# Product-key expert layer: four u tiles a head, v tiles prepared before the u sweep ends, first head's low parts off GpSimd

## The chip, the cores and the metric

The kernel runs on one core of one Trainium2 chip. The metric is the device time of one execution in microseconds. The core has a matrix engine (TensorE, PE in the rows; PEld is its weight load), VectorE (DVE), ScalarE (ACT), GpSimd (POOL) and a queue engine (SP) that issues most transfers; GpSimd issues the indirect ones (gathers).

## The reference

Two layers over 512 tokens of width 1024. Each layer has a mixer (convolution and gated linear attention, or forgetting attention) and then an expert part, which is what the change touches:

```python
q = (h @ wq).reshape(B, S, PEER_HEADS, 2, half)            # 8 heads, 2 halves of 128
s1, s2 = q[..., 0, :] . keys[:, 0], q[..., 1, :] . keys[:, 1]   # 128 scores each
v1, i1 = lax.top_k(s1, 16); v2, i2 = lax.top_k(s2, 16)
cand = (v1[..., :, None] + v2[..., None, :])               # 256 sums
sc, j = lax.top_k(cand, 16)
e1 = take(i1, j // 16); e2 = take(i2, j % 16)
experts = e1 * 128 + e2; gates = softmax(sc)
act = gelu(einsum('td,ted->te', ht, u[et]))                # 16384 experts, 128 used by a token
out = einsum('te,ted->td', gt * act, v[et])
```

## The kernel before, in words

The expert part computes three of the four token blocks densely: all 128 tiles of 128 experts of `u` against the tokens (the u sweep), then all 128 tiles of `v` (the v sweep), with a matrix G that holds each token's gate at its experts and zero elsewhere. Block 0 and the first 32 tokens of block 1 use gathers of single rows instead (`g_u`, `g_v`, and `x_u` for the 32 tokens). Each weight tile is loaded in float32 (`weight`, SP queue, 512 KB), ScalarE rounds it to a high part (L52), and the rest is subtracted into a low part (L53), on VectorE or, where `eng` says so, on GpSimd. Each product is three matmuls (L75 to L77).

The stages of an expert part, in order:

- the norm (`rms_body`): squares on ScalarE, a power on GpSimd (L104), the scaled rows on VectorE (L105), transposes on PE (L112);
- the route stage, a loop over 8 heads: two projections (`proj_T`), scores, then `route`, all top-16 searches on VectorE (`topk`, L740 to L745), then `WQU` = 3 u tiles (`u_step`). The last part of routing, `lookup`, turns positions into expert numbers with one-hot sums (L798 to L807); it is put one head later, behind the first u tile's low part. Every head past the first puts `XR` = 2 gathers `x_u` in motion, the last one 4. After the eighth head `gates` makes the softmax and E holds the expert numbers. GpSimd makes the low parts of both projections of head 0, of the second projection of every head, of u tiles 0 and 1, and of the odd u tiles from 13 on within this stage;
- the rest of the u sweep, 104 tiles: first `flip` transposes E and the gates on PE (L929), then every tile comes with one `gate4` of the 96 that build G (GpSimd, ScalarE and VectorE make one-hot rows, PE multiplies them, L959, and a copy goes to G in DRAM) and about 1.4 gathers. The gates end `TAIL` = 8 tiles before the end;
- the v sweep, 128 tiles: G is read back in pieces of eight tiles (`gc`, 1.5 MB), multiplied by the activations (L1083), split (`wh`, `wl`) and multiplied with `v` on PE (L1053). The first tile's preparation follows the last u tile and the gelu of the gathered dots (`g_w`).

A tile planner takes the program and sets each engine's order by a simulated time line; `issue_after(x)` puts instructions behind x on x's engine. Buffers bound how far one engine runs ahead: 4 raw tiles, 3 high and 3 low parts, 5 gathered rows.

Of the kernel before, what the change touches and what calls it, by code (L numbers as in the profile page):

```python
# [32 lines left out]
XR = 2  # L33
# [7 lines left out]
WQU = 3  # L41
# [5 lines left out]
class Trunk:  # L47
# [8 lines left out]
    def weight(self, src, shape=None, eng=None):  # L56
# [6 lines left out]
        self.split(raw, hi, lo, eng)  # L63
# [29 lines left out]
    def rms_body(self, rp, i, hT, h0, order, after, hx):  # L93
# [3 lines left out]
        def scale(b):  # L97
# [4 lines left out]
            nc.scalar.activation(sq, self.xb[b], AF.Square, accum_out=ss)  # L102
# [30 lines left out]
    def proj_T(self, src, hT, eng=None, between=None):  # L133

        wh, wl = self.weight(src, (KD, P), eng)
# [611 lines left out]
    def route(self, sb, s, E, SC, hd):  # L747
# [21 lines left out]
        def lookup():  # L769
# [4 lines left out]
            dx = sb.tile([P, 2, n, TOPK], BF16, name="dx")  # L774
            ixw = ix.rearrange("p b w k -> p w b k")
            for w in range(2):
                nc.vector.tensor_tensor(dx[:, w], ixw[:, w, :, 1:], ixw[:, w, :, 0:TOPK], op=ALU.subtract)
            wide = [P, 2 * n, TOPK, TOPK]
            st = sb.tile([P, 2 * n, TOPK * TOPK], BF16, name="st", tag="rs", bufs=2)
            nc.scalar.activation(st.rearrange("p b (r k) -> p b r k", k=TOPK),  # L780
                                 dx.rearrange("p w b r -> p (w b) r")[:, :, :, None].to_broadcast(wide), AF.Copy)
            jf = sb.tile([P, n, TOPK], F32, name="jf")
            nc.vector.tensor_copy(jf, j)


            pl = sb.tile([P, 2, n, TOPK], BF16, name="pl")
            nc.scalar.activation(pl[:, 0], jf, AF.Copy)
            bits = sb.tile([P, 3, n, TOPK], U32, name="bits")
            j2 = sb.tile([P, 3, n, TOPK], F32, name="j2")
            for k, (m, end) in enumerate(((3, 56.0), (4, 40.0), (8, 16.0))):  # L790
                nc.vector.tensor_scalar(bits[:, k], j, m, None, op0=ALU.bitwise_and)
                nc.vector.scalar_tensor_tensor(j2[:, k], jf, end, bits[:, k], op0=ALU.is_lt, op1=ALU.mult)
            nc.vector.tensor_tensor(j2[:, 0], j2[:, 0], j2[:, 1], op=ALU.add)
            nc.vector.tensor_tensor(pl[:, 1], j2[:, 0], j2[:, 2], op=ALU.add)

            oh = sb.tile([P, 2 * n, TOPK * TOPK], BF16, name="oh", tag="rs", bufs=2)
            for w in range(2):
                nc.vector.tensor_tensor(oh[:, w * n:(w + 1) * n].rearrange("p b (r k) -> p b r k", k=TOPK),  # L798
                                        pl[:, w, :, None, :].to_broadcast([P, n, TOPK, TOPK]),
                                        self.steps[:, w, None].to_broadcast([P, n, TOPK, TOPK]), op=ALU.is_ge)  # L800
            nc.vector.tensor_tensor(oh, oh, st, op=ALU.mult)

            for m in (1, 2, 4):
                pair = oh.rearrange("p b (r h m) -> p b r h m", h=2, m=m * TOPK)
                nc.vector.tensor_tensor(pair[:, :, :, 0, 0:TOPK], pair[:, :, :, 0, 0:TOPK], pair[:, :, :, 1, 0:TOPK],
                                        op=ALU.add)
# [417 lines left out]
```

## Time and profile before

| | us |
|---|---|
| median of 3 runs | 3182.42 |
| lowest and highest run | 3172.59, 3187.05 |
| profiled execution, its own time | 3180.49 |
| span in the profile | 3178.7 |
| PE busy | 3024.8 |
| DVE busy | 2466.8 |
| ACT busy | 1541.1 |
| POOL busy | 1394.1 |

The span runs from the first instruction to the last. Busy times overlap between engines. Matmuls are pipelined, and a busy PE at half of its clock still counts as busy, so the share of 95% does not by itself say that nothing is to be had. "Granted clock" is the share of PE's full 2.4 GHz.

### The profile page before, as it was taken

The page shows a single profiled execution, that of the slowest core. Times are in us where ns is not written, and L with a number is a line of the kernel's source. Part 1 is how long each engine was busy: PE and PEld are TensorE (multiplying, and loading weights), DVE is VectorE, ACT ScalarE, POOL GpSimd, SP SyncE. Part 2 cuts the span into 40 slices and gives each one's busy share as a digit, 9 for nine tenths or more (in the row PEclk, how much of TensorE's full clock was granted, in tenths as well). Part 3 has the DMA queues.
Part 4 walks back from the last instruction along what each step waited for, and adds up shares of the span by engine and source line. Part 5 has one row for each costly group of instructions (what it writes and reads, how often), then busy time and mean ns, then how long its engine had stood idle before and what let it go on. Part 6 is the DMA issues. An engine that isn't in the chain of part 4 may idle for free.

```text
span 3178.7 us, 46471 instructions
## 1 busy us (share of the span) xinstructions
PE 3024.8 (95%) x15934; PEld 2635.8 (83%) x15934; DVE 2466.8 (78%) x5338; ACT 1541.1 (48%) x2668; POOL 1394.1 (44%) x1072
## 2 busy tenths in 40 slices
PE   8999996999999999999999989969999999999999
PEld 6767886999999888887766669869999997887787
DVE  7764999888787888888546538998877888888886
ACT  4353334777765333333356624337667753333333
POOL 1321233999786233333100012328999983332330
PEclk9999997999999999999999999989999999999999
DMA  4104554999999999999421125558999999999996
GB/s 154 60 27 131 178 182 137 344 368 357 338 336 337 323 355 359 346 358 346 149 80 43 39 83 178 166 181 293 340 347 330 342 340 332 369 354 336 361 346 211
DMA packets 343808, 815.00 MB, mean 256 GB/s; under 512 B 27897, under 2 KB 182922, under 8 KB 337426
## 3 DMA queue, kind: packets, MB, share of 16 engines
q1 hardware_dynamic: 260626, 510.00, 46.2%
q0 software_dynamic: 82944, 302.03, 26.8%
q8 instruction: 125, 2.05, 0.3%
q14 instruction: 113, 0.93, 0.1%
HBM read 717.74 MB, written 93.06 MB: 255 GB/s over the span
## 4 chain that ended last, share of the span: by engine, by line
PE 74%; DVE 8%; DMA 2%; ACT 1%; issue 1%; POOL 0%; SPq 0%; DVEq 0%; ACTq 0%; POOLq 0%
PE acc L1053 32%; PE pu L75 9%; PE pu L77 9%; PE pu L76 9%; PE bank L959 5%; PE bank L77 2%; PE bank L75 2%; PE bank L76 2%; PE po L672 1%; PE bank L640 1%; DVE wlo L53 1%; DVE gr L897 1%; DVE tk L743 1%; DMA raw<-in_vF_dram 1%; ACT whi L52 1%
## 5 line engine op out<-in xcount | busy, mean ns | idle before, releaser
L52 ACT ACTIVATE whi<-raw 128x1024 fp32r<-128x1024 f32 x604 | 634.7, 1056 | 643.2 <-PE pu L76 310.6
L53 DVE TENSOR_TENSOR wlo<-raw,whi 128x1024 fp32r<-128x1024 f32 x565 | 693.0, 1227 | 194.8 <-ACT whi L52 193.8
L75 PE MATMUL pu<-hhi,whi 128*128 128x352 f32 x2048 | 687.1, 335 | 13.3 <-ACT xact L871 10.2
L77 PE MATMUL pu<-hhi,wlo 128*128 128x352 f32 x2048 | 671.8, 328 | 12.9 <-DVE wlo L53 11.9
L76 PE MATMUL pu<-hlo,whi 128*128 128x352 f32 x2048 | 669.3, 327 | 0.6 <-DVE hlo L115 0.6
L914 POOL DMA_INDIRECT gr<-in_vF_dram,ids x256 | 329.6, 1287 | 664.0 <-DVE x L916 620.2
L1053 PE MATMUL acc<-wlo,wh 128*128 128x512 f32 x1536 | 474.4, 390 | 0.0
L1053 PE MATMUL acc<-whi,wl 128*128 128x512 f32 x1536 | 471.7, 389 | 0.0
L1053 PE MATMUL acc<-whi,wh 128*128 128x512 f32 x1536 | 430.7, 392 | 24.1 <-ACT wh L52 13.8
L52 ACT ACTIVATE wh<-gc 128x384 fp32r<-128x384 f32 x256 | 134.2, 525 | 644.5 <-PE acc L1053 628.0
L879 POOL DMA_INDIRECT gr<-in_uN_dram,ids x256 | 406.3, 1587 | 83.3 <-issue 37.1
L942 POOL TENSOR_SCALAR a<-cst,sT 128x128 f32<-128x128 f32 x384 | 425.7, 1118 | 38.2 <-ACT sT L930 19.3
L75 PEld LDWEIGHTS pu<-hhi,whi 128*128 128x128 f32 x2048 | 391.6, 191 | 17.8 <-ACT xact L871 12.7
L77 PEld LDWEIGHTS pu<-hhi,wlo 128*128 128x128 f32 x2048 | 390.5, 191 | 14.4 <-DVE wlo L53 13.1
L76 PEld LDWEIGHTS pu<-hlo,whi 128*128 128x128 f32 x2048 | 391.5, 191 | 1.7 <-DVE hlo L115 0.9
L1053 PEld LDWEIGHTS acc<-whi,wh 128*128 128x128 f32 x1536 | 288.7, 189 | 88.4 <-ACT whi L52 14.6
L1053 PEld LDWEIGHTS acc<-wlo,wh 128*128 128x128 f32 x1536 | 289.8, 189 | 60.3
L1053 PEld LDWEIGHTS acc<-whi,wl 128*128 128x128 f32 x1536 | 288.6, 188 | 59.9
L916 DVE SCALAR_TENSOR_TENSOR x<-gr,dots,x 128x1024 f32<-128x1024 f32 x256 | 327.4, 1279 | 0.4
L881 DVE CUSTOM_DVE_ANT_0 gr<-gr,h 128x1024 f32<-128x1024 f32 x256 | 309.5, 1230 | 15.7 <-DMA gr<-in_uN_dram,ids 14.9
L53 POOL TENSOR_TENSOR wlo<-raw,whi 128x1024 fp32r<-128x1024 f32 x39 | 101.4, 2606 | 497.6 <-ACT whi L52 497.5
L53 DVE TENSOR_TENSOR wl<-gc,wh 128x384 fp32r<-128x384 f32 x256 | 141.9, 555 | 120.9 <-ACT wh L52 118.5
(264 smaller groups left out, 4529.4 us busy)
## 6 DMA issues: line engine op xcount, KB each, us to landing
raw<-in_uT_dram SPq DMA_DIRECT2D x256, 512.0 KB
raw<-in_vF_dram SPq DMA_DIRECT2D x256, 512.0 KB
G<-big SPq DMA_DIRECT2D x48, 1024.0 KB
gc<-G SPq DMA_DIRECT2D x32, 1536.0 KB
aside<-xact SPq DMA_DIRECT2D x208, 176.0 KB
at<-aside SPq DMA_DIRECT2D x104, 352.0 KB
raw<-in_w_in_dram SPq DMA_DIRECT2D x32, 512.0 KB
raw<-in_wq_dram SPq DMA_DIRECT2D x32, 512.0 KB
```

What stands on the lines that cost most here:

```text
L52: first = self.nc.scalar.activation(hi, raw, AF.Copy)
L53: self.last_lo = (eng or self.nc.vector).tensor_tensor(lo, raw, hi.bitcast(F32), op=ALU.subtract)
L75: mm(out, lh, rh, start=first, stop=False)
L76: mm(out, lh, rl, start=False, stop=False)
L77: return mm(out, ll, rh, start=False, stop=last)
L879: nc.gpsimd.indirect_dma_start(out=r, out_offset=None, in_=uN, in_offset=bass.IndirectOffsetOnAxis(ap=ids[:, s:s + 1], axis=0))
L881: return lambda: nc.vector.tensor_tensor_reduce(r, r, h0, 1.0, 0.0, ALU.mult, ALU.add, accum_out=dots[:, s:s + 1])
L914: nc.gpsimd.indirect_dma_start(out=r, out_offset=None, in_=vF, in_offset=bass.IndirectOffsetOnAxis(ap=ids[:, s:s + 1], axis=0))
L916: return lambda: nc.vector.scalar_tensor_tensor(self.x0, r, dots[:, s:s + 1], self.x0, op0=ALU.mult, op1=ALU.add)
L942: nc.gpsimd.tensor_scalar(a2[:, t], self.iota, e2[:, t:t + 1], None, op0=ALU.is_equal)
L959: nc.tensor.matmul(p[:, t], a2[:, t], a1[:, t], start=True, stop=True)
L1053: nc.tensor.matmul(acc[b][c], wt[:, s], vt[:, c], start=(n == 0 and wt is wh and vt is vh), stop=(n == NE1 - 1 and wt is wl))
```

## The change

Five edits, all in the expert part:

1. `WQU` 3 to 4: 32 instead of 24 u tiles go between the heads. `XR` 2 to 3, from head 0 on.
2. `lookup` is no longer a function put off by a head; its instructions follow the searches of their own head. The copies on ScalarE and GpSimd go (`ix`, `st`, `pl[0]`): VectorE takes differences of the expert numbers directly, copies `pl[0]` itself, and multiplies the one-hot matrix by the differences, read 16 times each from a stride of zero, where before it multiplied by `st`, which ScalarE had written out.
3. Head 0's projections and u tiles 0 and 1 have their low parts on VectorE. The high parts of head 0's projections are put behind the norm's last square on ScalarE.
4. `PLAIN` = 3: after the route stage come three u tiles without gates, then the `flip` transposes, then gates at 96 in 85 tiles. `QTAIL` = 3: the gathers for `u` end three tiles earlier than before.
5. When the gates are done, the buffers of the gate stage are given up and those of the v sweep opened, and the first transfers of the v sweep (`fetch`) are issued there. v tile 0 is prepared before the last u tile, v tile 1 behind it, both ahead of `g_w`.

```diff
-XR = 2
+XR = 3
-WQU = 3
+WQU = 4
+PLAIN = 3
+QTAIL = 3
...
-    def weight(self, src, shape=None, eng=None):
+    def weight(self, src, shape=None, eng=None, after=None):
...
+        if after:
+            with self.tc.issue_after(after.ins):
+                self.split(raw, hi, lo, eng)
+        else:
+            self.split(raw, hi, lo, eng)
...
-            nc.scalar.activation(sq, self.xb[b], AF.Square, accum_out=ss)
+            self.last_sq = nc.scalar.activation(sq, self.xb[b], AF.Square, accum_out=ss)
...
-            ix = sb.tile([P, n, 2, 1 + TOPK], BF16, name="ix")
-            nc.gpsimd.memset(ix[:, :, :, 0:1], 0.0)
-            nc.scalar.activation(ix[:, :, :, 1:], i1, AF.Copy)
...
-            nc.scalar.activation(st.rearrange("p b (r k) -> p b r k", k=TOPK),
-                                 dx.rearrange("p w b r -> p (w b) r")[:, :, :, None].to_broadcast(wide), AF.Copy)
...
-            nc.scalar.activation(pl[:, 0], jf, AF.Copy)
...
-            nc.vector.tensor_tensor(oh, oh, st, op=ALU.mult)
...
+        nc.vector.tensor_copy(dx[:, :, :, 0:1], ixw[:, :, :, 0:1])
+        nc.vector.tensor_tensor(dx[:, :, :, 1:], ixw[:, :, :, 1:], ixw[:, :, :, 0:TOPK - 1], op=ALU.subtract)
...
+        nc.vector.tensor_copy(pl[:, 0], jf)
...
+        nc.vector.tensor_tensor(ohs, ohs, dx.rearrange("p w b r -> p (w b) r")[:, :, :, None].to_broadcast(
+            [P, 2 * n, TOPK, TOPK]), op=ALU.mult)
...
-                    p = self.proj_T(A["wq"][L, 2 * hd + w], hT, nc.gpsimd if w or not hd else None)
+                    p = self.proj_T(A["wq"][L, 2 * hd + w], hT, nc.gpsimd if w and hd else None,
+                                    after=None if hd else self.last_sq)
...
-                lookups.append((self.route(rb, sd, E, S, hd), hd))
+                self.route(rb, sd, E, S, hd)
+                x_ids(hd)
+                xq.extend((x_u, (hd, c)) for c in range(XQ))
...
-                    lo, mm = u_step(nu, nc.gpsimd if nu < 2 or nu > 12 and nu % 2 else None)
+                    lo, mm = u_step(nu, nc.gpsimd if nu > 12 and nu % 2 else None)
...
-                rows = pump(xq, XR if hd < HEADS - 1 else 2 * XR)
-            found()
+                rows = pump(xq, XR)
...
+        first = nu + PLAIN
+        ng, nq = 4 * len(groups) / (NE1 - TAIL - first), len(gathers) / (NE1 - LAG - QTAIL - nu)
...
+        while nu < NE1:
+            if vb and nu == NE1 - 1:
+                ready.append(prepare(0))
+            lo, mm = u_step(nu)
+            nu += 1
...
+                if nu == first:
+                    for b in range(nd):
+                        flip(b)
...
+            if not (gates or products or vb):
+                upool.__exit__(None, None, None)
+                vb = vpool.__enter__()
+                for n in range(AHEAD):
+                    fetch(n)
...
+        ready.append(prepare(1))
         g_w()
...
-            for n, e in enumerate(order):
...
+        for n in range(NE1):
+            fetch(n + AHEAD)
+            lo, tile = ready.pop(0) if ready else prepare(n)
```

`fetch(n)` issues `gc` for every eighth tile and `at` (the activations kept in DRAM) for every second one past the first 24. `prepare(n)` is the body of the old v loop up to the split: the load and split of `v`, the product of G and the activations, and its split.

## Rows read from the trace of the kernel before

**Rows 1.** The page's slices: GB/s moved in each fortieth of the span.
```profile
...
GB/s 154 60 27 131 178 182 137 344 368 357 338 336 337 323 355 359 346 358 346 149 80 43 39 83 178 166 181 293 340 347 330 342 340 332 369 354 336 361 346 211
```

**Rows 2.** Busy time in four windows: route stage and u sweep, layers 0, 1.
```profile
...
285.98:541.90 255.92, 218.55 (x1144) 198.56 (x1144) 232.97 (x1066) 90.42 (x145) 66.53 (x47) 0.91 0.51 163
541.90:1027.30 485.40, 479.46 (x3195) 478.25 (x3193) 392.82 (x771) 335.17 (x676) 414.98 (x330) 1.00 0.93 339
1901.46:2149.30 247.84, 211.92 (x1151) 193.46 (x1150) 229.94 (x1062) 92.61 (x145) 65.26 (x46) 0.94 0.52 168
2149.30:2634.60 485.30, 482.33 (x3197) 481.52 (x3195) 390.15 (x768) 335.93 (x677) 438.12 (x328) 1.00 0.94 335
```

**Rows 3.** Waits of PE over the whole span: us in total, times, longest.
```profile
...
PE bank L929 <- DVE E L807: 32.4, 2, 16.3
```

**Rows 4.** Groups of DVE by line, layer 0, 304.6 to 541.3 us.
```profile
...
L53 DVE TENSOR_TENSOR wlo<-raw,whi 128x1024 fp32r<-128x1024 f32 x27 | 32.7, 1212 | 2.0 <-ACT whi L52 2.0
L897 DVE CUSTOM_DVE_ANT_0 gr<-gr,hx 128x1024 f32<-128x1024 f32 x21 | 25.2, 1223 | 3.6 <-DMA gr<-in_uN_dram,idx 3.6
...
L798 DVE TENSOR_TENSOR oh<-pl,steps 128x1024 bf16<-128x1024 bf16 x16 | 16.2, 1015 | 0.1
...
L805 DVE TENSOR_TENSOR oh<-oh 128x1024 bf16<-128x1024 bf16 x8 | 10.2, 1280 | 0.0
L801 DVE TENSOR_TENSOR oh<-oh,st 128x2048 bf16<-128x2048 bf16 x8 | 9.7, 1217 | 0.1
...
L783 DVE CAST jf<-j 128x64 f32<-128x64 uint32 x8 | 1.7, 210 | 0.2
```

**Rows 5.** Groups of POOL by line, the same stretch.
```profile
...
L53 POOL TENSOR_TENSOR wlo<-raw,whi 128x1024 fp32r<-128x1024 f32 x13 | 34.7, 2676 | 91.3 <-ACT whi L52 91.3
```

**Rows 6.** Timeline of POOL and DVE, layer 0, around 441 and 478 us.
```profile
...
440.59 2.37 POOL L53 TENSOR_TENSOR wlo<-raw,whi 128x1024 fp32r<-128x1024 f32 x1 [2.14 <-ACT whi L52]
...
441.37 2.14 DVE L798 TENSOR_TENSOR oh<-pl,steps 128x1024 bf16<-128x1024 bf16 x1
...
477.99 0.67 DVE L798 TENSOR_TENSOR oh<-pl,steps 128x1024 bf16<-128x1024 bf16 x1
```

**Rows 7.** Timeline of ACT: two u tiles without gates, layer 1.
```profile
...
2627.06 0.47 ACT L871 ACTIVATE act<-pu 128x352 f32<-128x352 f32 x1 [2.39 <-PE pu L77]
...
2630.86 0.47 ACT L871 ACTIVATE act<-pu 128x352 f32<-128x352 f32 x1 [2.39 <-PE pu L77]
```

**Rows 8.** Busy time in four short stretches where PE stands or runs slowly.
```profile
...
523.90:540.10 16.20, 0.12 (x2) 0.05 (x1) 15.75 (x76) 5.33 (x6) 1.07 (x2) 0.57 0.35 107
1027.30:1035.20 7.90, 0.04 (x2) 0.03 (x1) 3.92 (x7) 4.89 (x7) 1.74 (x2) 0.76 1.08 347
2634.60:2640.60 6.00, 0.07 (x2) 0.05 (x1) 3.62 (x8) 2.03 (x4) 2.89 (x2) 0.87 1.09 343
2640.60:2646.00 5.40, 5.40 (x13) 4.24 (x14) 3.80 (x9) 0.77 (x2) 0.00 (x0) 0.51 1.08 354
```

**Rows 9.** Timelines of POOL and DVE at the start of both expert parts.
```profile
...
269.57 8.02 POOL L53 TENSOR_TENSOR wlo<-raw,whi 128x1024 fp32r<-128x1024 f32 x3 [0.21 <-ACT whi L52]
277.53 0.57 POOL L104 TENSOR_TENSOR rs<-ss,sc 128x1 f32<-128x1 f32 x1
...
273.56 0.14 DVE L103 TENSOR_SCALAR ss<-ss 128x1 f32<-128x1 f32 x1
...
1886.15 2.35 POOL L53 TENSOR_TENSOR wlo<-raw,whi 128x1024 fp32r<-128x1024 f32 x1
...
1886.23 3.36 DVE L105 SCALAR_TENSOR_TENSOR xs<-x,rs,grow 128x1024 f32<-128x1024 f32 x1 [0.85 <-POOL rs L104]
...
1890.03 1.28 DVE L105 SCALAR_TENSOR_TENSOR xs<-x,rs,grow 128x1024 f32<-128x1024 f32 x1 [0.32 <-POOL rs L104]
```

**Rows 10.** Groups of POOL by line, whole span.
```profile
...
L942 POOL TENSOR_SCALAR a<-cst,sT 128x128 f32<-128x128 f32 x384 | 425.7, 1118 | 38.2 <-ACT sT L930 19.3 <-ACT whi L52 6.4 <-issue 4.9
L879 POOL DMA_INDIRECT gr<-in_uN_dram,ids x256 | 406.3, 1587 | 83.3 <-issue 37.1 <-DVE dots L881 35.4 <-DVE a L952 5.0
```

More of the change, by code (lines that the diff above doesn't have):

```diff
@@ L967, in peer_body @@
         nu = 0
-        xq, rows, lookups = [], [], []
-        def found():
-            f, hd = lookups.pop(0)
-            f()
-            x_ids(hd)
-            xq.extend((x_u, (hd, c)) for c in range(XQ))
+        xq, rows = [], []
         with tc.tile_pool(name=f"pr{L}", bufs=2, reuse_waits="tile") as rb:
@@ new lines, in prepare @@
+        def prepare(n):
+            e, r = order[n], n % EC
+            a = kept[e - (NE1 - KEEP)] if e >= NE1 - KEEP else ats[n - n % 2][:, n % 2]
+            vh, vl = self.weight(vN[e], (2, 512))
+            lo = self.last_lo
+            w = gcs[n - r][:, :, r * TG:(r + 1) * TG]
+            wd = w[:, TX // TG:]
+            nc.vector.tensor_tensor(wd, wd, a.rearrange("p (g t) -> p g t", t=TG), op=ALU.mult)
+            wh = vb.tile([P, TD], F32R, name="wh", bufs=3)
+            wl = vb.tile([P, TD], F32R, name="wl", bufs=3)
+            self.split(w, *[t.rearrange("p (g t) -> p g t", t=TG) for t in (wh, wl)])
+            return lo, (n, vh, vl, wh, wl)
@@ new lines, in peer_body @@
+        ready = []
+        groups = [(b, tg) for b in range(nd) for tg in range(P // TG)]
+        groups = groups[TX // TG:] + groups[0:TX // TG]
+        gathers = xq + [(g_u, (s,)) for s in range(SLOTS)]
+        nx = len(xq)
+        first = nu + PLAIN
+        ng, nq = 4 * len(groups) / (NE1 - TAIL - first), len(gathers) / (NE1 - LAG - QTAIL - nu)
+        cg = cq = 0.0
+        products, rows = [], [rows] + [[] for _ in range(LAG - 1)]
+        upool = tc.tile_pool(name=f"pu{L}", bufs=2, reuse_waits="tile")
@@ new lines, in peer_body @@
+        vpool = tc.tile_pool(name=f"pv{L}", bufs=2, reuse_waits="tile")
+        ub, vb = upool.__enter__(), None
+        gates = [(gate4, (ub, b, tg, g)) for b, tg in groups for g in range(TG // 4)]
+        while nu < NE1:
[3 more added lines that the diff above has]
+            nu += 1
+            with tc.issue_after(mm.ins):
+                for f in products:
+                    f()
+                if nu == first:
+                    for b in range(nd):
+                        flip(b)
+            products = []
+            if nu >= first:
@@ new lines, in peer_body @@
+        for n in range(NE1):
+            fetch(n + AHEAD)
+            lo, tile = ready.pop(0) if ready else prepare(n)
+            tail.append(tile)
+            if n < NE1 - 3:
+                for b in range(nd):
+                    v_sweep(tail, b)
+                tail.clear()
+            with tc.issue_after(lo.ins):
+                for f in rows.pop(0):
+                    f()
+            cq += nq
+            rows.append(pump(gathers, cq))
+            cq -= int(cq)
+            if not gathers and not any(rows) and not done:
+                done = True
+                g_end()
@@ L1101, in peer_body @@
+        vpool.__exit__(None, None, None)
         assert done
```

151 lines of the change are left out of this document (47 added, 104 removed).

## The prediction, made before the result was known

> **What bounds the kernel now.** I read the page first. Its slices of bytes [rows 1] show the two expert parts as the two long runs above 320 GB/s, so the time lies there, and the change touches nothing else. Then I asked for busy time by stage [rows 2]. A row gives the stretch, its length, the busy us of PE, PEld, DVE, ACT and POOL, the granted clock, the DMA share and GB/s. The reader is to see two kinds of stage. In the u sweep PE is busy for 479 and 482 of 485 us at full clock, and VectorE only for 392: PE sets the pace. In the route stage VectorE is busy for 233 of 256 and 230 of 248 us, while PE has 218 and 212 at a mean clock of 0.91 and 0.94: VectorE sets the pace, and PE both stands and falls to its lower level. The waits of PE name where this ends: twice 16 us for E, the last thing that routing writes [rows 3]. In that gap VectorE is busy for 15.75 of 16.2 us [rows 8]. So the route stage ends when VectorE has worked off its list, and what matters is the length of that list and how many u tiles PE has behind it by then.
>
> **Eleven u tiles leave the u sweep.** Eight go between the heads, three more run ahead of `flip`. A tile without gates takes 3.80 us on PE, from the distance of two gelus [rows 7], so a layer's u sweep shrinks by 11 x 3.80 = 41.8 us. The 96 gates stay. PE can take them in the route stage: 218.5 busy us, part of it at half clock, plus 41.8 are 260, against 256 plus the growth that follows.
>
> **VectorE's list before E grows.** Its parts, for a layer:
>
> - Low parts. The window holds 27 [rows 4]: 7 first projections (heads 1 to 7), 16 of the 24 u tiles, 4 run ahead. After the change 7 projections and, of u tiles 2 to 34, the 23 that GpSimd does not have make 30, and I take 2 ahead: 32, so 5 x 1.21 = 6.1 us. With none or 4 ahead it is 3.6 to 8.5.
> - The dot products `x_u`. Three a head instead of two, from head 0 on: 21 are in the window [rows 4], I take 25, 4 x 1.22 = 4.9 us. Bounds: none, and all 32 (13.4 us).
> - GpSimd's low parts. The two engines hold each other up: an `oh` comparison of 1024 elements takes 0.67 us alone and 2.14 us when GpSimd subtracts at its side [rows 6]. Over the window the 16 comparisons and the 8 first folds of that size cost 26.4 instead of 24 x 0.67 = 16.1 us [rows 4], 10.3 us for the 13 low parts of GpSimd [rows 5], 0.8 each. Head 0's leave, but the odd u tiles from 13 to 31 are 10 instead of 6: 7 + 10 = 17 in the window. For 4 more I take 1 us each, as short operations pay too: 4 us. Bounds 3.2 and 4 x 2.68 = 10.7.
> - The one-hot multiply. With `st` written out it takes 1.22 us for 2048 elements [rows 4]. Now one operand repeats each value 16 times from a stride of zero. No row shows that. Below it is 1.22 as now; above it is the float32 subtraction, 1.21 us for 1024 elements, so 2.42. I take the upper end, since both fast bfloat16 rows (L798, L801) read neighbouring values on each side, and this operand has none: 8 x 1.21 = 9.6 us.
> - The copies from ScalarE. One of 64 elements a head comes over, 8 x 0.21 = 1.7 us by the cast L783 [rows 4]. The two differences become a copy and a difference, taken as equal.
>
> Together 26.3 us; the low ends give 8.5, the high ends 43.9. That ScalarE and GpSimd lose `ix`, `st` and `pl[0]` I cost at nothing: ScalarE is busy for 90 of 256 us there [rows 2].
>
> One rule of the Trainium skill speaks against the multiply: "VectorE: DVE Perf Modes", section "Mode 2×_1P — pack two bf16 into one 32-bit read", wants 16-bit operands with a step of ±1 for two elements a cycle. Its tier table gives 1224 ns for 2048 bf16 elements of such an operation and 2293 ns where the fast mode is out. The old multiply's 1217 ns agrees with the first figure; no run here shows the second. By the rule a layer loses 8.6 us in this term and the sum is 2 us lower than mine; by the old row alone it would be 19 us lower.
>
> Net for a layer: 26.3 - 41.8 = -15.5 us, bounds -33.3 and +2.1.
>
> **The start.** In layer 0 the norm's sum of the last block is there at 273.70, but its power waits until 277.53 behind three low parts on GpSimd, 3.8 us. In layer 1 the scaling at 1886.23 takes 3.36 instead of 1.28 us while GpSimd subtracts, 2.1 us more [rows 9]. Both go. VectorE gets four low parts for it, 4 x 1.21 = 4.8 us, in a stretch where it otherwise waits for transposes. I take 4 us for both layers together; bounds 0 and 5.9.
>
> **The seam.** Between the last u and the first v matmul PE stands for 7.9 and 6.0 us, and behind the second gap it runs 5.4 us at a clock of 0.51, a loss of 2.6 [rows 8]: 16.5 us in all. With two v tiles ready only `g_w` and the third tile's high part come behind, covered by two tiles of matmuls. What prepare adds ahead of the last u tile (a load, two roundings, a product, two subtractions) falls where no gates run. On SP, `gc` (1.5 MB) now stands ahead of the last raw tiles and waits for the last write of G; behind it wait the loads of u tiles and of v tiles 0 and 1. Up to four raw tiles are loaded by then, so I leave 2.5 us and take 14; bounds 0 and 16.5.
>
> **The u sweep gets denser.** It moves 339 x 485 us = 165 MB now [rows 2]. Eleven tiles with their stores (0.69 MB each) and 4 gathers (0.5 MB) less, one `gc` more, are 157 MB in 443.5 us, 354 GB/s. Slices of 79 us reach 368 and 369 [rows 1], so it can be moved, with less air. If it stayed at 339 GB/s it would be 463 us, 20 more. I take 4 us a layer; bounds 0 and 20.
>
> **Sum.** 2 x (-15.5) - 4 - 14 + 2 x 4 = -41 us. From the profiled execution's own 3180.5 us that is 3139.5. That execution lay 1.9 us under the median, so I predict 3141 us.
>
> **The rivals.**
>
> 1. *Light list.* The multiply keeps its speed and the other low ends hold: growth 8.5 us, 2 x (-33.3) - 4 - 14 + 8 = -77, 3106 us. For it: the planner may let few `x_u` ahead. Against it: the stride of zero.
> 2. *The list eats the tiles.* VectorE's list grows by the whole 41.8 us (GpSimd's 17 low parts hold VectorE at their full length). Then start, seam and density are left: -10 us, 3172. For it: the route stage is already VectorE's. It decides from a growth of 42 us on.
> 3. *The seam stays.* `gc` comes late, or the raw loads queued behind it do, and the gap moves instead of closing: -27 us, 3155. For it: both happen on one queue.
> 4. *Slower: GpSimd becomes the bound of the u sweep.* It is busy for 415 and 438 of 485 us there [rows 2], with two comparisons of 1.12 us a gate and gathers of 1.59 us each [rows 10]. The gates now come at 96 in 85 tiles. If that is real work, the sweep can lose only four gathers, 6.4 us, and stays at 479 instead of 443.5 us: 2 x 35.5 = +71 in place of the density's 8, so +22 us, 3204. It decides from where a tile's GpSimd work exceeds its PE work. Against it: layer 0 does the same work in 23 us less than layer 1, and PE nowhere waits for it, so much of that time is waiting inside the instructions.
>
> **How the numbers follow.** Chances: the sum as worked out 0.50, seam stays 0.10, light list 0.12, list eats the tiles 0.18, GpSimd bound 0.10. About 0.5%, 16 us, is what a measurement of this kernel can tell from no change. The first three are faster by more, with a small part of the sum's upper end taken off: 0.71. The case at 3172 is the same: 0.19. GpSimd's is slower: 0.10. The forecast alone spans 3120 to 3160. The range that leaves out 2 in 10 cuts half of the light list and most of GpSimd's case: 3100 to 3186.
>
> **What would show it.** In the profile after: `flip` some 26 us later than 540 and 2148, with 35 tiles behind it; the multiply near 2.4 us; about 32 low parts and 25 `x_u` in front of E; 17 low parts on GpSimd there; `flip` to the last u matmul near 447 us; gaps at the seam under 2 us with no fall of the clock; the powers of the norm right behind their sums. I am wrong if `flip` comes over 40 us later, if PE waits for a GpSimd comparison in the u sweep, or if the last u tiles wait for their raw loads.

## The result: slower by 0.65%

The changed kernel takes 3201.7 us (median of 6 runs) beside 3180.7 us for the kernel before, a ratio of 1.0065 with a 95% interval of 1.0049 to 1.0082. It is 21 us slower where 41 us faster was forecast, and lies above the range. The profiled execution spans 3202.7 us, that of before 3178.7. Cut at four marks a layer, the 24.0 us between the two lie here (layers 0 and 1; u sweep: first `flip` matmul to the end of the last u matmul; seam: from there to the first v matmul; v sweep: first to last v matmul):

| us | before | after | change | forecast |
|---|---|---|---|---|
| to `flip` (layer 1: from the last v matmul of layer 0) | 540.1, 584.3 | 576.7, 615.9 | +68.2 | +48.6 |
| u sweep | 487.2, 486.7 | 461.6, 466.3 | -46.0 | -75.6 |
| seam | 7.9, 6.0 | 8.6, 1.0 | -4.3 | -14.0 |
| v sweep | 528.4, 533.0 | 534.9, 532.6 | +6.1 | 0 |

Every line came out worse than forecast, and none of them alone turns the sign. Busy time by stage of the changed kernel answers [rows 2]: route stage, u sweep and v sweep of layer 0, route stage and u sweep of layer 1, then the 6 us behind one of PE's stalls and the middle 400 us of the v sweep of layer 0.

```profile
...
285.98:576.70 290.72, 256.30 (x1380) 234.17 (x1378) 268.14 (x1085) 88.30 (x139) 78.89 (x45) 0.94 0.51 171
576.70:1038.30 461.60, 448.33 (x2962) 445.95 (x2962) 371.39 (x749) 322.35 (x658) 396.49 (x326) 0.98 0.93 332
1046.90:1581.80 534.90, 527.13 (x2304) 434.05 (x2305) 432.67 (x525) 193.59 (x264) 167.30 (x128) 0.99 0.95 331
1919.50:2197.70 278.20, 242.48 (x1331) 223.51 (x1329) 263.34 (x1083) 83.94 (x134) 76.87 (x45) 0.96 0.52 173
2197.70:2664.00 466.30, 455.56 (x2962) 453.48 (x2962) 375.36 (x756) 323.18 (x658) 390.43 (x328) 0.98 0.94 335
657.62:663.50 5.88, 5.88 (x22) 5.79 (x23) 3.19 (x9) 2.69 (x7) 5.21 (x6) 0.50 0.96 351
1100.00:1500.00 400.00, 393.36 (x1729) 323.89 (x1729) 330.69 (x391) 142.78 (x193) 135.54 (x104) 1.00 1.00 352
```

VectorE is busy for 268 of 291 and 263 of 278 us of the route stage, so the list still sets its end, and the list is longer. The u sweep is another stage than before: PE is busy for 448 and 456 us, not for nearly all of it, and the mean clock is 0.98. The waits of PE over the whole span (us in total, times, longest) answer [rows 3]. Three more rows of the kernel before come first, then the changed kernel's:

```profile
...
PE pu L77 <- DVE wlo L53: 11.9, 4, 6.0
...
PE pu L75 <- ACT xact L871: 10.2, 8, 2.5
...
PE bank L77 <- DVE wlo L53: 4.3, 3, 3.1
```

```profile
...
PE bank L83 <- DVE wlo L55: 29.1, 10, 5.0
PE pu L83 <- DVE wlo L55: 26.2, 17, 3.1
...
PE pu L81 <- ACT xact L868: 14.1, 6, 3.5
...
PE bank L926 <- DVE E L806: 12.9, 2, 6.9
PE bank L956 <- POOL a L939: 9.6, 9, 2.9
PE acc L1082 <- ACT wh L54: 9.5, 2, 8.6
```

The wait for E fell from 32.4 to 12.9 us, as the tiles ahead of `flip` should make it. In its place PE waits 55 us for VectorE's low parts in the route stage (16 before), 9.6 us for GpSimd's comparisons (never before) and 14.1 us for gelu results (10.2 before). In the u sweep of layer 0 these two are:

```profile
...
PE pu L81 <- ACT xact L868: 7.2, 4, 3.5
...
PE bank L956 <- POOL a L939: 5.9, 4, 2.9
```

VectorE's groups in layer 0 up to `flip` (304.6 to 576.7 us), and GpSimd's low parts there, answer [rows 4, 5]:

```profile
...
L894 DVE CUSTOM_DVE_ANT_0 gr<-gr,hx 128x1024 f32<-128x1024 f32 x28 | 46.8, 1673 | 6.1 <-DMA gr<-in_uN_dram,idx 6.1
L55 DVE TENSOR_TENSOR wlo<-raw,whi 128x1024 fp32r<-128x1024 f32 x33 | 41.7, 1264 | 1.8 <-ACT whi L54 1.8
L799 DVE TENSOR_TENSOR oh<-oh,dx 128x2048 bf16<-128x2048 bf16 x8 | 18.3, 2282 | 0.1
...
L795 DVE TENSOR_TENSOR oh<-pl,steps 128x1024 bf16<-128x1024 bf16 x16 | 10.9, 684 | 0.2
...
L778 DVE TENSOR_TENSOR dx<-i 128x120 bf16<-128x120 uint32 x8 | 7.2, 896 | 0.0
...
L804 DVE TENSOR_TENSOR oh<-oh 128x1024 bf16<-128x1024 bf16 x8 | 6.4, 804 | 0.1
...
L55 POOL TENSOR_TENSOR wlo<-raw,whi 128x1024 fp32r<-128x1024 f32 x17 | 44.2, 2597 | 112.1 <-ACT whi L54 112.0
```

The multiply takes 2.28 us. The dot products are 28, not 25, and their mean is 1.67 us instead of 1.22. The comparisons fell to 0.68 us, so GpSimd's hold has moved from them to the dot products and to the differences of the expert numbers (L778), which take 0.27 us at their shortest and 0.90 in the mean.

A stall of the u sweep in the timelines of GpSimd, VectorE and PE (start, duration, engine, operation, idle time before):

```profile
...
650.01 3.14 POOL L939 TENSOR_SCALAR a<-cst,sT 128x128 f32<-128x128 f32 x2
...
654.43 3.73 POOL L939 TENSOR_SCALAR a<-cst,sT 128x128 f32<-128x128 f32 x2
...
661.61 1.21 POOL L939 TENSOR_SCALAR a<-cst,sT 128x128 f32<-128x128 f32 x2
...
650.41 1.21 DVE L55 TENSOR_TENSOR wlo<-raw,whi 128x1024 fp32r<-128x1024 f32 x1
651.54 1.21 DVE L878 CUSTOM_DVE_ANT_0 gr<-gr,h 128x1024 f32<-128x1024 f32 x1
...
653.68 1.21 DVE L55 TENSOR_TENSOR wlo<-raw,whi 128x1024 fp32r<-128x1024 f32 x1
654.81 1.21 DVE L878 CUSTOM_DVE_ANT_0 gr<-gr,h 128x1024 f32<-128x1024 f32 x1
...
655.96 1.21 DVE L878 CUSTOM_DVE_ANT_0 gr<-gr,h 128x1024 f32<-128x1024 f32 x1
...
657.62 2.25 PE L956 MATMUL bank<-a,a 128*128 128x128 f32 x8 [2.94 <-POOL a L939]
```

Two comparisons take 1.21 us at 661.61, but 3.14 and 3.73 us while VectorE runs low parts (L55) and dot products. PE waits 2.94 us for them, and in the 5.9 us behind the wait its granted clock is 0.50 (the row from 657.62 in the windows above).

The seam of layer 0, on SP's queue and VectorE:

```profile
...
1012.76 0.33 SPq L959 DMA_DIRECT2D G<-big  x1
...
1023.19 0.33 SPq L62 DMA_DIRECT2D raw<-in_uT_dram  x1
...
1026.20 0.39 SPq L1009 DMA_DIRECT2D gc<-G  x1
...
1045.79 3.57 DVE L1022 TENSOR_TENSOR gc<-gc,act 128x352 f32<-128x352 f32 x8 [7.37 <-DMA gc<-G]
```

The last u raw load waits 9.4 us for a buffer until 1023.19, `gc` is issued behind it at 1026.20, and VectorE can take it at 1045.79; PE stood from 1038.4 to 1046.9.

### The profile page after: what moved, and what is told of

Its sections match the earlier page's. It is cut to its first block, busy times and chain, and to the rows that moved or that the text cites. A ratio compares the mean times of both kernels' runs of the same rounds, so it can differ in the third digit from the quotient of the medians.

```text
span 3202.7 us, 46577 instructions
## 1 busy us (share of the span) xinstructions
PE 3045.0 (95%) x15934; PEld 2649.2 (83%) x15934; DVE 2506.5 (78%) x5354; ACT 1459.9 (46%) x2586; POOL 1338.3 (42%) x1056
## 4 chain that ended last, share of the span: by engine, by line
PE 77%; DVE 9%; issue 5%; DMA 4%; POOL 3%; ACT 1%; SPq 0%; DVEq 0%; POOLq 0%; ACTq 0%
PE acc L1082 32%; PE pu L81 7%; PE pu L82 7%; PE pu L83 7%; PE bank L956 5%; PE bank L83 4%; PE bank L81 4%; PE bank L82 4%; DMA gr<-in_uN_dram,idx 2%; DVE wlo L55 2%; DMA gc<-G 1%; DVE gr L894 1%; PE pc L291 1%; PE po L678 1%; PE bank L646 1%
## 5 line engine op out<-in xcount | busy, mean ns | idle before, releaser
L55 DVE TENSOR_TENSOR wlo<-raw,whi 128x1024 fp32r<-128x1024 f32 x565 | 694.4, 1229 | 201.9 <-ACT whi L54 188.1
L81 PE MATMUL pu<-hhi,whi 128*128 128x352 f32 x2048 | 689.4, 337 | 17.0 <-ACT xact L868 14.1
L1082 PE MATMUL acc<-whi,wh 128*128 128x512 f32 x1536 | 412.8, 391 | 24.6 <-ACT whi L54 15.0
L876 POOL DMA_INDIRECT gr<-in_uN_dram,ids x256 | 388.6, 1518 | 97.1 <-DVE dots L878 53.5
L939 POOL TENSOR_SCALAR a<-cst,sT 128x128 f32<-128x128 f32 x384 | 381.7, 1003 | 32.5 <-ACT whi L54 17.7
L55 DVE TENSOR_TENSOR wl<-gc,wh 128x384 fp32r<-128x384 f32 x256 | 141.8, 555 | 130.6 <-ACT wh L54 130.5
L83 PE MATMUL bank<-hhi,wlo 128*128 128x512 f32 x512 | 208.3, 407 | 29.1 <-DVE wlo L55 29.1
```

The lines of the kernel that those rows point to most:

```text
L55: self.last_lo = (eng or self.nc.vector).tensor_tensor(lo, raw, hi.bitcast(F32), op=ALU.subtract)
L81: mm(out, lh, rh, start=first, stop=False)
L83: return mm(out, ll, rh, start=False, stop=last)
L876: nc.gpsimd.indirect_dma_start(out=r, out_offset=None, in_=uN, in_offset=bass.IndirectOffsetOnAxis(ap=ids[:, s:s + 1], axis=0))
L939: nc.gpsimd.tensor_scalar(a2[:, t], self.iota, e2[:, t:t + 1], None, op0=ALU.is_equal)
L1082: nc.tensor.matmul(acc[b][c], wt[:, s], vt[:, c], start=(n == 0 and wt is wh and vt is vh), stop=(n == NE1 - 1 and wt is wl))
```

## The experiments

The kernel before ran beside each on the same chip. Its median went from 3178 to 3193 us over the experiments, so ratios to it are compared; 0.001 is 3.2 us, and the difference of two ratios is uncertain by 0.0022 to 0.004. Times of one stage come from one profiled execution each, and they scatter: the run without every other gather of v rows, below, edits the v sweeps alone, and yet its first `flip` came 4.1 us earlier than the changed kernel's, its u sweeps took 467.8 and 458.3 us for 461.6 and 466.3, and its seams 3.1 and 10.0 us for 8.6 and 1.0. A difference of that size in one stage shows nothing by itself. Unless another base is named, "against the changed kernel" is against its 1.0065.

### VectorE's list

**The lookup's copies back on ScalarE.**
```diff
-        nc.vector.tensor_copy(pl[:, 0], jf)
+        nc.scalar.activation(pl[:, 0], jf, AF.Copy)
...
-        nc.vector.tensor_tensor(ohs, ohs, dx.rearrange("p w b r -> p (w b) r")[:, :, :, None].to_broadcast(
-            [P, 2 * n, TOPK, TOPK]), op=ALU.mult)
+        nc.vector.tensor_tensor(oh, oh, st, op=ALU.mult)
```


> The changed kernel with the lookup of before written in line: ScalarE makes ix, st and pl[0] again, and the one-hot multiply reads st. Theory 1 (VectorE's list sets the end of the route stage, and the multiply is one of its long terms): the multiply falls from 2.28 to 1.22 us, 8 times a layer, the copies of pl and dx go back to ScalarE, so flip comes 9 to 12 us earlier in each layer and the kernel takes 3178 to 3184 us instead of 3202. Rival (the list has room, or the way through ScalarE is waited for head by head now that the lookup is not put off behind a u tile): flip moves by under 4 us a layer, 3195 us or more.

Measured 0.9983 (0.9967 to 0.9999), 26 us under the changed kernel; `flip` 10.7 us earlier in layer 0 and 11.0 in layer 1. The list theory holds. The multiply took 1.50 us in the mean there, the comparisons 0.96: some of the hold moved back to them.

**Two dot products a head.**
```diff
-XR = 3
+XR = 2
```


> The changed kernel with two dot products x_u a head instead of three. Theory 1 (list): seven of the 28 x_u leave the window before E, at 1.2 us alone and 1.67 us as they were measured beside GpSimd's subtractions, so flip comes 9 to 20 us earlier a layer; the u sweep takes the eight gathers back. VectorE has 90 us of air there, so the kernel gains what flip gains, 3165 to 3185 us. Rival (GpSimd is what makes the u sweep late): eight more gathers of 1.2 to 1.6 us on GpSimd lengthen the sweep by 10 to 13 us a layer, and the sum stays within 6 us of 3202.

Measured 0.9968 (0.9948 to 0.9988), 31 us under the changed kernel. `flip` came 7.5 and 10.0 us earlier; eight gathers more in the u sweep did not lengthen it (459.5 and 450.3 us), which speaks against a sweep that is bounded by all that GpSimd has to do. The list theory holds in kind: layer 0 stays under its 9 to 20 us, and `flip` gives 17.5 of the 31 us.

**The u tiles' low parts on VectorE.**
```diff
-                    lo, mm = u_step(nu, nc.gpsimd if nu > 12 and nu % 2 else None)
+                    lo, mm = u_step(nu)
```


> The changed kernel with the low parts of the u tiles in the route stage all on VectorE, none on GpSimd; the second projections of heads 1 to 7 stay on GpSimd. It prices the hold that GpSimd's subtractions have on VectorE. If one holds VectorE for 0.8 to 1 us, as the sum of the forecast had it, VectorE's list grows by 10 x (1.2 - 0.9) = 3 us a layer: 3204 to 3212 us. If VectorE is held for the whole of the 2.4 us: the list shortens by 12 us a layer, 3178 to 3186 us.

Measured 1.0002 (0.9985 to 1.0019), 20 us under the changed kernel, `flip` 13.1 and 8.6 us earlier. VectorE's groups in layer 0 up to `flip`:

```profile
...
L55 DVE TENSOR_TENSOR wlo<-raw,whi 128x1024 fp32r<-128x1024 f32 x43 | 53.5, 1245 | 1.1 <-ACT whi L54 1.1
L894 DVE CUSTOM_DVE_ANT_0 gr<-gr,hx 128x1024 f32<-128x1024 f32 x28 | 35.5, 1288 | 2.7 <-DMA gr<-in_uN_dram,idx 2.7
```

Ten low parts more cost 11.8 us, the dot products gave back 11.3. From 293 us to `flip` VectorE was busy for 258.6 instead of 267.2 us, so ten subtractions of GpSimd had held it for 11.8 + 8.6 = 20.4 us, 2.0 us each, not the 1 us of the forecast. This is layer 0; in layer 1 `flip` moved by the same 8.6 us.

### The moved tiles

**Three tiles a head again, the rest kept.**
```diff
-WQU = 4
+WQU = 3
```


> The changed kernel with three u tiles a head instead of four; the three tiles ahead of flip and all else stay. Theory 1 (a moved tile still saves its 3.8 us in the sweep and costs VectorE 1.2 to 2.4 us in the list): eight tiles fewer in the route make flip 10 to 19 us earlier and the sweep 30 us longer, so the kernel gets 20 to 40 us slower, 3222 to 3242 us. Rival (the route stage pays for a moved tile what the sweep saves, since PE has no time there, and the gates come thicker): flip 25 to 30 us earlier, sweep 25 to 30 us longer, 3196 to 3208 us.

Measured 1.0127 (1.0104 to 1.0149), 20 us over the changed kernel: given the rest of the change, the move pays, at the lower end of the theory. `flip` came 14.1 us earlier in layer 0 and 1.1 in layer 1, the u sweep took 27.1 and 22.5 us longer. The 1.1 us fits neither theory.

**Four tiles a head alone, in the kernel before.**
```diff
-WQU = 3
+WQU = 4
```


> The kernel before with four u tiles a head instead of three, and no other edit. Theory 1 (a tile moved into the route costs VectorE 1.2 to 2 us there and saves 3.8 us in the sweep; with three tiles a head the changed kernel lost 21 us): eight tiles give 2 x 8 x (1.8 to 2.6) us less 10 to 16 us for thicker gates, 96 in 88 tiles, so 3140 to 3168 us. Rival (without the rest of the change the route has no room for them): 3176 to 3190 us.

Measured 0.9983 (0.9966 to 1.0001): nothing that counts, the rival. The u sweep gave 27.8 and 28.4 us. The way to `flip` took 15.9 and 23.3 of it, the seam 3.4 and 2.1, the v sweep 8.7 and 5.1.

**Old lookup, two dot products and later products together.**
```diff
-XR = 3
+XR = 2
...
+        nc.vector.tensor_tensor(oh, oh, st, op=ALU.mult)
...
-            a2 = ub.tile([P, 4, P], F32, name="a2", bufs=3)
+            a2 = ub.tile([P, 4, P], F32, name="a2", bufs=5)
```


> The changed kernel with the old lookup on ScalarE, two dot products a head, and the products of a gate one tile later, all three together; the tile move, the head-0 edit and the preparing ahead stay. Theory 1 and 2 (list and gates are separate costs that add): 25 us, 28 us and 14 us below 3202, so 3130 to 3142 us, flip near 558 and 2135 us with 35 tiles done. Rival (they lift the same limit: once flip is earlier, PE has too little behind it in the route and only waits longer for E): not much under the best of the three, 3155 to 3172 us.

Measured 0.9966 (0.9947 to 0.9985), the rival: three gains of 26, 31 and 13 us give 31 together. `flip` came at 565.5 us, no earlier than with the lookup alone (566.0), while PE waited 18.8 us for E instead of 12.9. The v sweeps took 535.7 and 542.3 us.

### The u sweep

**Products one tile later.**
```diff
-                products = pump(gates, cg)
+                held = pump(gates, cg)
...
+            products, held = held, []
```


> The changed kernel with the products of a gate group issued one u tile later (five buffers for each comparison instead of three), so that GpSimd's two comparisons have one more tile of time. Theory 2 (the gates now come at 96 in 85 tiles, a tile with two of them makes GpSimd's comparisons late, and PE stands for them or for the gelu queued behind the copy of the product, then runs on at the lower clock): the 5.9 and 7.2 us of waits in layer 0 and 3.7 and 6.9 us in layer 1 go, with the half clock behind them, and the kernel takes 3170 to 3182 us. Rival (the waits come from the transfers or from PE's own order): under 6 us gained, 3196 us or more.

Measured 1.0025 (1.0010 to 1.0040), 13 us under the changed kernel; the sweep went to 453.4 and 460.0 us. Half of what the theory said, and short of its range.

**Every other load of a u tile left out.**
```diff
+        if again:
+            raw = self.last_raw
+        else:
...
+            wh, wl = self.weight(uT[e], (KD, P), eng, again=e > 36 and e % 2 == 1 and e < NE1 - 2)
```


> The changed kernel without the load of every other u tile behind flip (tiles 37, 39 and so on to 125, 45 a layer, 23 MB): such a tile is worked out from the raw tile before it, so its output is another; every instruction of PE, VectorE, ScalarE and GpSimd stays. Theory 3, formed from the runs so far: from flip to the last v matmul every kernel moves 332 to 336 GB/s, so the two sweeps take what their bytes take. Then the u sweep falls from 461.6 and 466.3 us to PE's own 440 to 447, and the kernel to 3160 to 3175 us. Theory 2 alone (GpSimd's comparisons and the gates' order make PE stand): the sweep stays within 8 us of 461, the kernel above 3188 us.

Measured 1.0129 (1.0109 to 1.0150): theory 3 falls for the u sweep. Its windows of both u sweeps:

```profile
...
575.00:1036.00 461.00, 448.30 (x2938) 443.00 (x2938) 372.75 (x754) 319.62 (x655) 414.28 (x329) 0.99 0.85 291
2206.70:2663.10 456.40, 443.42 (x2938) 438.94 (x2938) 373.86 (x756) 317.35 (x655) 407.32 (x329) 0.99 0.87 296
```

PE's waits in that of layer 0:

```profile
...
PE bank L960 <- POOL a L943: 11.9, 15, 1.9
```

The bytes fell from 332 to 291 GB/s and the sweep stayed; PE now met GpSimd's comparisons 15 times instead of 4, for 11.9 us instead of 5.9. Why the whole kernel got 20 us slower is not settled: the v sweeps took 543.7 and 543.0 us, with 14.6 us of waits for v low parts.

**One of GpSimd's two comparisons of a gate on VectorE.**
```diff
-                nc.gpsimd.tensor_scalar(a2[:, t], self.iota, e2[:, t:t + 1], None, op0=ALU.is_equal)
+                (nc.vector if t else nc.gpsimd).tensor_scalar(a2[:, t], self.iota, e2[:, t:t + 1], None, op0=ALU.is_equal)
```


> The changed kernel with the second of GpSimd's two comparisons of each gate on VectorE; nothing else moves. Without every other load the u sweep moved 293 instead of 332 GB/s and stayed at 461.0 and 456.4 us, with 27 waits for GpSimd's comparisons, 24 us: so the transfers do not set it. Theory 2 (GpSimd sets it: 192 comparisons and 128 gathers are 400 us of 461): half of the comparisons gone, the sweep falls to PE's own 440 to 450 us and the kernel to 3165 to 3182 us, although VectorE has 27 us more to do. Rival (PE's order or VectorE sets it): the sweep stays within 6 us of 461 and 466, 3196 us or more.

Measured 0.9941 (0.9921 to 0.9960), 39 us under the changed kernel by the ratios and 32 by the medians, the most of any single edit. Both u sweeps, then PE's waits in that of layer 0, and the first `gc` on SP's queue:

```profile
...
573.30:1028.80 455.50, 447.49 (x2962) 445.61 (x2962) 387.03 (x847) 321.81 (x658) 267.99 (x230) 0.99 0.94 340
2180.20:2627.00 446.80, 437.40 (x2962) 436.09 (x2962) 388.82 (x854) 321.46 (x659) 280.40 (x233) 0.99 0.96 351
```

```profile
...
PE pu L81 <- ACT xact L868: 7.2, 4, 3.5
PE bank L956 <- POOL a L939: 0.8, 3, 0.4
```

```profile
...
1012.43 0.39 SPq L1009 DMA_DIRECT2D gc<-G  x1
```

GpSimd is busy for 268 instead of 396 us, PE's waits for its comparisons in layer 0 fell from 5.9 to 0.8 us, and the sweep is 6.1 and 19.5 us shorter. That the edit pays is clear of noise in the kernel's time; how much of it falls to each sweep is not, since 6.1 us is within the scatter and the run with two dot products a head had 450.3 us in layer 1 without it. Only layer 1 reached the theory's 440 to 450 us. PE's waits for gelu stayed, 7.2 us in layer 0, so these are not GpSimd's comparisons. Both seams are closed (1.1 and 1.0 us): in layer 0 `gc` was issued 16.4 us ahead of the last u matmul's end instead of 12.2.

### The v sweep

**Every other load of a v tile left out.**
```diff
+        vh, vl = self.weight(vN[e], (2, 512), again=n > 1 and n % 2 == 1)
```


> The changed kernel without the load of every other v tile (63 a layer, 33 MB; such a tile is worked out from the raw tile before it, so its output is another), all instructions of the engines kept. Theory 3 (bytes): in the v sweep the transfer engines are busy for 1.00 of the middle 400 us and PE for 391 to 397; without the bytes the sweep falls from 534.9 and 532.6 us to PE's own length, 522 to 527 by its 2304 matmuls of 0.227 us, and the waits for whi go: 3180 to 3190 us. Rival (the v sweep is PE's as it stands): within 5 us of 3202.

Measured 1.0198 (1.0177 to 1.0220), with v sweeps of 557.6 and 542.9 us. It tells nothing of the transfers' share: a new wait came, 83 us of VectorE in layer 0 for `gc`, where the changed kernel has 3.8.

**Every other gather of a v row left out.**
```diff
+            if s % 2:
+                r = self.last_gr
+            else:
```


> The changed kernel without every other gather of v rows (64 a layer, 33 MB; the sum takes the row before again, so the output is another). It asks again what bounds the v sweep, without touching the queue of SP, where the run without loads made the loads of gc late. If the transfers do (1.00 of the middle 400 us): the sweep falls from 534.9 and 532.6 us to 522 to 527, 3178 to 3190 us, and the waits for whi go. Rival (PE's own work does): within 5 us a layer, 3194 us or more.

Measured 0.9957 (0.9942 to 0.9972), 34 us under the changed kernel by the ratios. The v sweeps took 526.8 and 526.0 us, 8.1 and 6.6 us less, so most of the 34 us lies elsewhere. The middle 400 us of layer 0:

```profile
...
1100.00:1500.00 400.00, 399.19 (x1761) 330.12 (x1760) 331.20 (x399) 148.44 (x196) 93.21 (x53) 1.00 0.88 290
```

With 0.88 of DMA time instead of 1.00 (windows above) PE is busy for 399 instead of 393 of 400 us. So the changed kernel's v sweep is bounded by its transfers, but only by some 7 us above PE's own length: in the kernel before the same 400 us of layer 0 had a DMA share of 1.01 and PE was busy for 397.

### The seam and the start

**Preparing ahead alone, in the kernel before.**
```diff
+            if vb and nu == NE1 - 1:
+                ready.append(prepare(0))
...
+        ready.append(prepare(1))
```


> The kernel before with the first two v tiles prepared inside the u sweep, and no other edit; gates stay at one in each tile. If the preparing closes the seam, the 7.9 and 6.0 us of standing and the half clock behind them go, 3166 to 3172 us. Rival (gc lands when it lands: its load cannot start before the last write of G, it takes 10 to 20 us, and behind the u and v loads on the queue of SP it is late again, as the 8.6 us of the changed kernel's layer 0 show): the seam stays in at least one layer, 3174 to 3184 us.

`QTAIL` = 3 comes with it. Measured 0.9946 (0.9924 to 0.9967), 17 us under the kernel before, a little more than the first theory said, with seams of 3.7 and 1.1 us. The two seams account for 9 us of the 21 between the two profiled executions; the u sweeps are 11 us shorter, the way to layer 1's `flip` 9, and the v sweeps 9 longer. So the gain is shown, but not that all of it is the seam's.

**The same with three tiles ahead of `flip`.**
```diff
-PLAIN = 0
+PLAIN = 3
```


> The kernel before with the first two v tiles prepared inside the u sweep, and three u tiles without gates ahead of flip; no other edit of the change. The three tiles lie in the 16 us in which PE waits for E. By PE's time they save 3 x 3.8 us a layer, 3138 to 3145 us; by theory 3 they save their bytes, 2.1 MB or 6 us a layer, and VectorE pays 1.2 us for those whose low part it takes ahead of E, so 3150 to 3158 us. Rival (the gates, 96 in 93 tiles instead of one in each, lose it again): 3159 to 3168 us.

Measured 0.9983 (0.9967 to 0.9999), 12 us over the run before it: the rival, past its upper end. Three tiles fewer are 11.4 us, but the u sweeps went from 481.0 to 486.2 and from 481.6 to 477.0 us, so 16.6 and 6.8 us were lost in them and the seams were back at 6.6 and 6.5 us; the 6.8 us and the seams are within the scatter. The density of the gates does not explain it: four tiles a head alone, with 96 gates in 88 tiles, lost 2.6 and 2.0 us of its 30.4. What the three tiles do to the order is open.

**Head 0 and u tiles 0 and 1 off GpSimd alone.**
```diff
-                    p = self.proj_T(A["wq"][L, 2 * hd + w], hT, nc.gpsimd if w or not hd else None)
+                    p = self.proj_T(A["wq"][L, 2 * hd + w], hT, nc.gpsimd if w and hd else None,
+                                    after=None if hd else self.last_sq)
...
-                    lo, mm = u_step(nu, nc.gpsimd if nu < 2 or nu > 12 and nu % 2 else None)
+                    lo, mm = u_step(nu, nc.gpsimd if nu > 12 and nu % 2 else None)
```


> The kernel before with only head 0 taken off GpSimd (its low parts go to VectorE, the first behind the last square). If the four microseconds that the first projections come earlier are kept to flip: 3176 to 3179 us. If VectorE's four more low parts of 1.2 us in the list before E eat them, which the route stage's being VectorE's list says: 3181 to 3186 us.

Measured 1.0011 (0.9991 to 1.0031): no change that can be told. A gain of 4 us, a ratio of 0.9987, lies just below the interval.

### Versions that beat both kernels

**Preparing ahead, the u tiles' low parts on VectorE.** The kernel before with `prepare` and with `u_step(nu)` in the route stage.

> The kernel before with the preparing ahead, and the low parts of all u tiles of the route stage on VectorE; those of the second projections and of head 0 stay on GpSimd. If GpSimd's subtraction holds VectorE for its whole length, about 2.4 us, as the run with low parts moved showed for the changed kernel: six low parts in the window give 6 x 1.2 = 7 us a layer, 3143 to 3152 us. If the hold is 0.8 to 1 us, as the forecast had it: 3160 to 3167 us.

Measured 0.9860 (0.9840 to 0.9881). Against 0.9946 for the preparing alone this is 27 us more by the ratios and 12 by the medians, so the price at full length or above it; `flip` came 10.6 and 8.9 us earlier. In layer 1 the u sweep took 496.1 us for 481.6, and the profiled execution is 9.4 us shorter, less than `flip` gained.

**The projections' low parts too.**
```diff
-                    p = self.proj_T(A["wq"][L, 2 * hd + w], hT, nc.gpsimd if w or not hd else None)
+                    p = self.proj_T(A["wq"][L, 2 * hd + w], hT)
```


> The same with the projections' low parts on VectorE too, so that GpSimd subtracts nothing in the route stage. Hold of the whole length: 13 low parts in the window give 13 x 1.2 = 16 us a layer, 3125 to 3138 us, and the comparisons of 1024 elements take 0.67 us each. Hold of 0.8 to 1 us: the list grows by 4 us a layer, 3165 to 3172 us.

Measured 0.9902 (0.9883 to 0.9921), 13 us worse than the run before it, where the price at full length would have made it better. The comparisons did fall to 0.68 us, but `flip` came 6.5 us later in layer 0 and PE waited up to 28.5 us for E. The seven subtractions of the projections do not cost what those of the u tiles do. Worked out from the timeline of the run before, each VectorE row beside a GpSimd subtraction against the same instruction without one, they lengthened VectorE's list by about 6 us in layer 0 and 3 in layer 1, and VectorE needs 7 x 1.22 = 8.5 us to take them over. They run mostly beside top-16 searches, and a search (MAX8) takes 0.28 us there as alone.

**With one comparison of a gate on VectorE as well.** The first of the three versions, and the edit of the gates.

> The kernel before with the preparing ahead, the u tiles' low parts in the route stage on VectorE, and the second GpSimd comparison of each gate on VectorE. With one gate in each tile PE hardly waited for GpSimd in the kernel before (u sweep 487 us, PE busy for 481), so theory 2 gives little here: 0 to 5 us a layer, a ratio of 0.983 to 0.987 against the 0.986 without this edit. Rival (GpSimd's clumps cost the sweep of the kernel before as much as the changed one's): 10 us a layer or more, a ratio under 0.981.

Measured 0.9888 (0.9857 to 0.9918), a little above the range of theory 2: no gain, as it said for one gate in each tile, or a small loss.

**The changed kernel with the found costs taken out, tiles still moved.** Old lookup, two dot products, `u_step(nu)`, and the edit of the gates.

> The changed kernel, with its eleven tiles moved, its head-0 edit and its preparing ahead, without the costs that the runs found: the lookup on ScalarE again, two dot products a head, the u tiles' low parts on VectorE, one of GpSimd's two comparisons of a gate on VectorE. If the move of the tiles pays once VectorE's list and GpSimd are free: flip near 555 us, a u sweep of 443 to 450 us, a closed seam, so 25 us less than the changed kernel's route and 30 us less in the sweeps' and seam's terms, a ratio of 0.972 to 0.984. Rival (PE has no time for eleven tiles in the route stage, and what the u sweep gains the v sweep gives back to its transfers): flip no earlier than 563 us, a v sweep of 535 to 542 us, a ratio of 0.988 to 0.995, behind the version without moved tiles.

Measured 0.9856 (0.9829 to 0.9883), on one chip with the version before it and not distinguishable from it. `flip` came at 556.4 us against 526.0, and the last u matmul of layer 0 ended at 1017.8 against 1018.4 us, so eleven tiles had moved for nothing there; in layer 1 they gave 18 us. The v sweeps were 544.8 and 541.5 us against 533.4 and 531.9. `flip` is the theory's, the v sweeps are the rival's, and the ratio lies between the two. Whether the move is worth anything stays open: 0.3%, uncertain by 0.4%.

## Why the prediction was wrong

**VectorE's list, +68.2 instead of +48.6 us with the start.** That the list sets `flip` was right (three runs). The multiply was sized right: 8.6 us against 9.6. The Trainium skill, "VectorE: DVE Perf Modes", section "The perf-mode tier table (the rule you actually need)", gives 2293 ns for a `tensor_tensor` of 2048 elements in the 1× mode, and the trace measures 2282. The low parts came out at 33 for 32. The step that failed is GpSimd's hold, "4 more I take 1 us each". It was read from the excess of comparisons and folds alone, 10.3 us, but the hold falls on whatever VectorE runs: in the changed kernel on the dot products above all, 28 x 0.45 = 12.6 us in layer 0. Measured by the run that takes them away, a u tile's subtraction costs 2.0 us. Counted over all rows of the timelines (each row beside a subtraction against the same instruction's median without one), GpSimd's subtractions lengthened the list by about 17 and 15 us before and by 28 and 24 after: 12 and 9 us more, where the sum had 4 a layer and a bound of 10.7. The second miss is the count of dot products, 28 for 25, 3.7 us a layer; the third is the start. The three are 24 us for the 20 that are missing, less 2 for the multiply. The Trainium skill, "SBUF — State Buffer", section "Who interferes with whom", says that a VectorE instruction with two SBUF inputs contends with a GpSimd instruction that reads SBUF, and calls the pair of ports that they share an exclusive lock; the trace agrees, with dot products of 2.38 us in the mean beside a subtraction and 1.21 without one in layer 0. The projections' subtractions, beside searches, had no such price in the run that moved them to VectorE.

**The u sweep, -75.6 becoming -46.0.** A tile's 3.80 us is not what failed: eight tiles alone gave 27.8 and 28.4 of 30.4 us. "I take 4 us a layer" for the denser sweep did: it was 16 and 21 us, at or past the bound of 20, and for another reason than transfers. Half of the loads away left the sweep where it was. GpSimd's comparisons come late where gathers, VectorE's low parts and its dot products meet them; in the stall shown PE stands 2.9 us and runs on at half clock. That is my second sign of error ("if PE waits for a GpSimd comparison") and a weaker form of rival 4: GpSimd does not bound the sweep as a whole, which took 462 and 466 us and not 479, with GpSimd busy for 396 and 390, and which eight more gathers did not lengthen, but it is late at single tiles. I had argued against rival 4 from PE's never waiting for GpSimd, which was true of that kernel only. Two runs that give the comparisons more room made the kernel 13 and 39 us faster. Of the two sweeps' 37 us, the profile with one comparison moved away has 26 back, of which 6 are within the scatter, and layer 1 of the run with two dot products a head shows 16 without that edit; the rest, waits for gelu among it, was not taken apart, and the run with three tiles ahead of `flip` suggests that part of it comes with the three tiles ahead of `flip`.

**The seam, -14.0 becoming -4.3.** Alone the edit gave 17 us, so the term was about right for the kernel before, in part by luck: only 9 us of it lie in the seams. In the changed kernel layer 0 is rival 3's case: `gc` stands on SP's queue behind a u load that waits for a buffer. With one comparison on VectorE the seam closed, but the run without every other gather of v rows had 3.1 us in layer 0 without that and 10.0 in layer 1, so how wide a seam is in one execution is in part chance.

**The v sweep, not in the sum, +6.1.** It is bounded by its transfers. All of the 6.1 us lies in layer 0, where 125 gathers for v fall into its time instead of 123; at the price below that is 3 us, and the rest is open. In the kernels with moved tiles and two dot products, 130 or so gathers fall in its time (131 with four tiles a head alone) instead of 123, some 0.5 MB each at 352 GB/s, 1.5 us, so 10 us of what the u sweep gains come back. The count is the trace's; that these gathers are the cause is worked out, not tried.

**The start, -4.** Not to be seen: head 0 and u tiles 0 and 1 alone measured no change. `flip` came 3.5 us earlier in layer 0 of that profile and 2.1 later in layer 1.

Rival 4 named the time, 3204 us, by luck. It was right for one part of its reason, but put all of the 63 us on the u sweep: three terms had to go wrong together, by 20, 30 and 10 us, with 6 from the v sweep.

## What to carry to other kernels

Where one engine's list sets a stage, price a neighbour's instructions by the whole list of a run with and without them, not by the one kind of row in which their hold shows now: the hold moves to other rows. Work taken out of a stage changes which engine is just in time there, so one that is busy for 0.85 of it is a candidate for the next bound even if nothing waits for it yet. And a gain ahead of a stage that is bounded by transfers has to be followed to the end of that stage.

## What was not expected of the hardware

- A GpSimd subtraction of 1024 elements (2.4 to 2.6 us) lengthened VectorE's list by 2.0 us where dot products ran beside it, and by under 1 us beside top-16 searches. Two comparisons of 128 elements on GpSimd, 1.21 us alone, took 3.73 us beside VectorE's low part and dot products: each engine holds up the other.
- After PE had stood for 2.94 us its granted clock was 0.50 over the next 5.9 us, so a 3 us stall costs about 6.
- A multiply with one operand repeated from a stride of zero ran at 2.28 us for 2048 bfloat16 elements, against 1.22 with both operands written out.
